# A planned two-layer trunk on one core: latest times, a tie and cold lengths in the plan of the instruction order

## The chip, the cores and the metric

The kernel runs on 1 core of a Trainium2 chip. The metric is the device time of one execution in microseconds (us). Before the change it is 809.21 us, the median of 3 runs (808.96 to 809.29).

## The reference

Two pre-norm residual layers over a sequence of 256 tokens with 1024 channels, all in float32. In each layer one wide projection of the normalised stream feeds three causal token mixers (a Mamba-2 scan, a sliding-window attention with sinks, a forgetting attention). Each mixer's result is projected to 1024 channels, gated and summed. One more projection is added to the residual, and a last RMS norm closes the trunk:

```
for layer in range(DEPTH):                                  # DEPTH = 2
    h = rms_norm(x, norm_w[layer])
    proj = einsum('bsd,de->bse', h, w_in[layer])
    ... split proj: inputs of the three mixers, their gates, the merge gates
    y_a = mamba2_branch(...); y_b = sliding_window_branch(...); y_c = forgetting_attention_branch(...)
    branch = einsum('bsiw,iwd->bsid', stack([y_a, y_b, y_c]), w_proj[layer])
    g = sigmoid(gates + gate_bias[layer])
    x = x + einsum('bsd,de->bse', sum(g * branch), w_out[layer])
return rms_norm(x, final_norm_w)                            # x * rsqrt(mean(x*x) + 1e-6) * w
```

## The kernel before, in words

**Work.** Every large product runs as three fp32r matmuls: each operand is split into a high part (`hi`, a rounding copy on ScalarE) and a remainder (`lo`, a subtraction on VectorE), and high times high, low times high and high times low are summed in PSUM. The 256 tokens are two halves of 128, `t` = 0 and 1. Weights come in parts of 512 KB from HBM on SyncE's queue into `raw`, are split into `hi` and `lo`, and are used once. TensorE's order is the order of the program text and is never changed.

**The plan.** The kernel is not issued as it is written. `Recorder` (line 199) takes down every operation with what it reads and writes, and `Op.cost` (line 159) gives it a length and a lag. `order_of` (line 276) then makes the order of each engine in 7 rounds. A round has two halves. `deadlines` (line 333) goes backwards: every operation gets a latest time `late` and a latest start `due`, from those that need it. A matmul's latest time is its `nominal` time. An operation that nothing on TensorE needs, such as the output's, has its own: `min(op.cap, end + 50.0)` in plan units (meant as us), line 335. `run` (line 351) goes forwards: whenever an engine is free, it takes, of the operations that could begin first, the one with the earliest `due`. `guarded` (line 413) looks whether a more urgent operation becomes ready before the chosen one would be over, and if so the engine takes something short or waits; line 440 uses it only from 16 units on (`OPENING`). The best round by its end is kept, and `emit` (line 498) issues it. So lengths and due times decide only an order; the times on the chip follow from that order and from semaphores.

**Loads are held.** A load without inputs that is not a weight part (line 305) is bound, in the first round, to the matmul that stands `LEAD` = 20 units ahead of its due time, and may not begin earlier in any round.

**The opening.** The program loads `x` half by half, transposes it on TensorE (`turn`, line 1912), and starts the first products. Two groups of transpositions of the identity, 7 (line 1899) and 10 (line 1967), keep TensorE occupied until the data come. In the plan a transposition is 0.109 long. `sum_sq` (line 700) takes the squares from which the first layer's row factor comes; the first projections' evictions are scaled by this factor.

**The end.** In the last layer `u_out2` (line 1653) multiplies the first 256 output columns for both halves, and `u_out` (line 1646) the rest, half by half (512 columns, then 256). `out_end` (line 1670) adds the residual on VectorE, sums the squares, and multiplies the piece by the final norm's weights and -0.5 (line 1687). With the last piece of a half, `row_rsqrt2` (line 711) makes the row factor by a square root on ScalarE, a reciprocal and a refining step on VectorE. Columns 0 to 640 are scaled by it on VectorE and leave on SyncE's queue; the others are scaled on ScalarE and leave on its queue (lines 1694 to 1699). `load_final` (line 1726) loads the weights, broadcast to 128 partitions (512 KB), on ScalarE's queue. The square root needs another activation table than the gates before it. Line 1662 therefore issues a dummy square root into `tab`; `last_of` (line 232) makes it wait for every ScalarE operation recorded before it, loads on ScalarE's queue included. Nothing waits for `tab`.

Of the kernel before, what the change touches and what calls it, by code (L numbers as in the profile page):

```python
# [13 lines left out]
AF = mybir.ActivationFunctionType  # L14
# [36 lines left out]
ENG = mybir.EngineType  # L51
ENGINES = ("tensor", "vector", "scalar", "gpsimd", "sync")
FIRST_WRITES = ("out", "accum_out")
SLIP, OPENING, LEAD = 0.3, 16.0, 20.0


class Buf:
# [79 lines left out]
class Op:  # L137

    def __init__(self, i, engine, name, args, kw):
        self.i, self.engine, self.name, self.args, self.kw = i, engine, name, args, kw  # L140
        self.ins = self
        self.deps, self.behind, self.after, self.bufs = set(), set(), [], []
        views = [("out" if k == 0 else "", a) for k, a in enumerate(args)] + list(kw.items())
        views = [(k, a) for k, a in views if isinstance(a, View)]
        self.writes = [a for k, a in views if k in FIRST_WRITES]
        self.reads = [a for k, a in views if k not in FIRST_WRITES]
        if name == "copy_predicated" or kw.get("accum_op") is not None:
            self.reads += self.writes
        sizes = [a.free_size() for _, a in views] or [1]
        self.cap, self.held = 1e9, False  # L150
        self.dma = name == "dma_start"
        self.n = max(sizes[0:1] if self.dma or engine == "tensor" else sizes)
        if self.dma:
            near = [a for _, a in views if a.buf.on_p][0]
            self.kb = near.shape[0] * near.free_size() / 256
            self.away = 6.0 if engine == "gpsimd" else 5.0
        self.cost()
# [41 lines left out]
class Recorder:  # L199
# [32 lines left out]
    def last_of(self, engine, op):  # L232

        op.deps.update(o.i for o in self.ops if o.engine == engine and o is not op)

    def access(self, op, v, writes):
        b = v.buf
# [38 lines left out]
def order_of(rec, bufs_of, rounds=7, verbose=False):  # L276

    ops = rec.ops
    by_tag = {}
    for b in rec.bufs:  # L280
        by_tag.setdefault(b.tag, []).append(b)
    for op in ops:
        op.behind = [d for d in op.behind - op.deps if ops[d].engine != "tensor" or op.engine != "tensor"]
        op.deps = sorted(op.deps)
        for d in op.deps:
            ops[d].after.append((op, True))
        for d in op.behind:
            ops[d].after.append((op, False))
    before = {}
    for tag, bs in by_tag.items():  # L290
        n = bufs_of[tag]
        for a, b in zip(bs, bs[n:]):
            before[id(b)] = a
    pe = [op for op in ops if op.engine == "tensor"]
    t = 0.0
    for op in pe:
        op.nominal, op.early = t, 0.0
        t += op.busy
    end, best = t, None
    for n in range(rounds):  # L300
        deadlines(ops, before, end)
        if not n:
            at = [op.nominal for op in pe]
            for op in ops:
                if op.dma and not op.deps and op.bufs and op.bufs[0].tag != "raw" and op.due > 10.0:
                    x = pe[bisect.bisect(at, op.due - LEAD) - 1]
                    op.behind.append(x.i)
                    op.held = True
                    x.after.append((op, False))
        end, before = run(ops, by_tag, bufs_of)  # L310
        t = late = last = 0.0
        for op in pe:
            gap, last = op.start - last, op.end
            if op.start > OPENING and gap > 0.03:
                late += gap
                if n > 1:
                    op.early += gap + 0.3
            t = op.start if op.start < OPENING else t
            op.nominal = t
            t += op.busy  # L320
        if best is None or end < best[0]:
            best = (end, [(op.start, op.end) for op in ops], [b.slot for b in rec.bufs])
        if verbose:
            print("round", n, "end", round(end, 2), "late", round(late, 2))
        end = t + 8.0
    for op, (op.start, op.end) in zip(ops, best[1]):
        pass
    for b, b.slot in zip(rec.bufs, best[2]):
        pass
    return sorted(ops, key=lambda op: (op.start, op.i))  # L330


def deadlines(ops, before, end):
    for op in ops:
        op.late = op.nominal + op.busy if op.engine == "tensor" else min(op.cap, end + 50.0)
    for op in reversed(ops):
        op.due = op.late - op.busy
        if op.engine == "tensor":
            op.due = min(op.nominal, op.due) - op.early
        for d in op.deps:  # L340
            o = ops[d]
            o.late = min(o.late, op.due - (o.away if o.dma else o.lag))
        for b in op.bufs:
            a = before.get(id(b))
            if a is not None:
                for o in a.users:
                    if o.i < op.i:
                        o.late = min(o.late, op.due - (o.away if o.dma else o.lag))


def run(ops, by_tag, bufs_of):
# [21 lines left out]
    forced = False  # L373
# [39 lines left out]
    def guarded(e, t0, op):  # L413

        k = 0
        for u in soon[e]:
            if u.due >= min(op.due, t0 + op.busy) or k == 6:
                return None
            if u.start is None and u is not op:
                k += 1  # L420
                r = max(ready_by(u), t0)
                if r < t0 + op.busy and t0 + op.busy > u.due + SLIP:
                    return r
        return None

    while done < len(ops):
        best = None
        for e in ENGINES:
            if e == "tensor":
                if at == len(pe) or pe[at].left:  # L430
                    continue
                c = [(when(pe[at]), pe[at])]
            else:
                c = [(when(op), op) for op in queues[e]]
            c = [(max(r, free[e]), op) for r, op in c if r is not None]
            if not c:
                continue
            t0 = min(r for r, _ in c)
            r, op = min(((r, op) for r, op in c if r <= t0 + 1e-9), key=lambda x: (x[1].due, x[1].i))
            if e != "tensor" and not forced and t0 > OPENING:  # L440
                until = guarded(e, t0, op)
                if until is not None:
                    c = [(r, op) for r, op in c if r + op.busy <= until + 0.02 or op.due < until]
                    if not c:
                        continue
                    t0 = min(r for r, _ in c)
                    r, op = min(((r, op) for r, op in c if r <= t0 + 1e-9), key=lambda x: (x[1].due, x[1].i))
            if best is None or r < best[0]:
                best = (r, e, op)
        if best is None and forced:  # L450
            raise RuntimeError("no operation can begin")
        forced = best is None
        if forced:
            continue
        r, e, op = best
        op.start, op.end = r, r + op.busy
        free[e] = op.end
        if op.dma:
            early = op.start < OPENING
            now, c = op.end + 0.8, op.kb / (330 if early else 300)  # L460
# [55 lines left out]
def hybrid_trunk(  # L516
# [8 lines left out]
    nc = Recorder()  # L525
# [18 lines left out]
    act = nc.scalar.activation  # L544
# [99 lines left out]
    tab = T("tab", [P, 1])  # L644
# [21 lines left out]
    ones = onesr.bitcast(F32)  # L666
# [44 lines left out]
    def row_rsqrt2(v, last):  # L711

        r0 = T("sm", [P, 8])
        if last:
            s = T("sm", [P, 8])
            act(s[:, 0:1], v, AF.Sqrt)
            nc.vector.reciprocal(r0[:, 0:1], s[:, 0:1])
        else:
            nc.gpsimd.tensor_tensor(r0[:, 0:1], v, mhalf[:, 0:1], op=ALU.pow)
        a = T("sm", [P, 8])  # L720
        stt(a[:, 0:1], r0[:, 0:1], v, r0[:, 0:1], op0=ALU.mult, op1=ALU.mult)
        r = T("rs", [P, 8], bufs=4)
        stt(r[:, 0:1], a[:, 0:1], -3.0, r0[:, 0:1], op0=ALU.add, op1=ALU.mult)
        return r
# [21 lines left out]
    def pin(f):  # L746
        return f
# [54 lines left out]
    ops = []  # L802
# [3 lines left out]
    first, late = [], []  # L806
# [846 lines left out]
    def u_out2(y, c):  # L1653

        def f(w):
            def late():
                drain(8)
                limit(None, True)
            drain(7)
            if y.l + 1 == L:  # L1660

                nc.last_of("scalar", pin(act)(tab, ones[:, 0:1], AF.Sqrt))
            xo = [out_start(y, c, t, 0, w.n) for t in range(2)]
            none = lambda: None
            for t, p in enumerate(tok2(y.mh, y.ml, w, (none, late, none, none))):
                out_end(y, c, t, 0, w.n, xo[t], p)
            state["pin"] = False
        return f
# [41 lines left out]
    fin = {}  # L1710
# [181 lines left out]
    if True:  # L1892
# [110 lines left out]
        v = T("sm", [P, 8])  # L2003
# [57 lines left out]
```

## Time and profile before

| what | value |
|---|---|
| median of 3 runs | 809.21 us |
| the profiled execution's own time | 809.29 us |
| its span, first to last instruction | 807.6 us |
| TensorE busy | 795.6 us, 99% |
| VectorE busy | 683.3 us, 85% |
| ScalarE busy | 542.3 us, 67% |
| GpSimd busy | 172.0 us, 21% |
| granted TensorE clock, mean | 0.997 |

How to read the profile's lines: a row of the timeline has the start in us from the span's start, the length in us, the engine, the line of the kernel, the operation, its output and input tiles with their shapes, and how many such instructions stand in a row (x2). In brackets stands how long the engine was idle before it, and what ended that. PE is TensorE's matmul, PEld its weight load, DVE VectorE, ACT ScalarE, POOL GpSimd, SP SyncE; a q behind the name marks the engine's queue, as for the issue of a transfer. All operations carry line 511, the line in `emit` that issues them, so they are told apart by their tiles: `raw`, `hi` and `lo` are weight parts, `mm` and `mx` PSUM banks, `rs` a row factor, `tab` the dummy root's tile, `L` one of the many buffers of common sizes. A row of a group has the count, then the busy time in us and the mean of one in ns.

### The profile page before, as it was taken

To read this page: it belongs to the slowest core of one execution; us is meant where nothing else is said; L and a number is where in the kernel's file an instruction comes from. 1 tells how busy PE (TensorE), PEld (TensorE's weight loads), DVE (VectorE), ACT (ScalarE), POOL (GpSimd) and SP (SyncE) were. 2 spreads that over 40 slices of the span, in tenths; PEclk is the share of its full clock that TensorE was granted. 3 is DMA by queue.
4 is the path that set the end of the run, shared out by engine and by line. 5 is a ranking of instruction groups with operands and counts; after the bars stand their busy time and mean duration, and the time that the engine had idled before them with its cause. 6 is when DMAs were issued, how large, how long until landed. Compare 5 with 4: busy or idle time off the path is not lost.

```text
span 807.6 us, 14854 instructions
## 1 busy us (share of the span) xinstructions
PE 795.6 (99%) x5160; PEld 711.8 (88%) x5160; DVE 683.3 (85%) x1416; ACT 542.3 (67%) x1146; POOL 172.0 (21%) x236
## 2 busy tenths in 40 slices
PE   8999999999999999999999999999999999999995
PEld 8998988888998988888999899888889899888894
DVE  6878999898899996797676889999988999869864
ACT  7876877776766885545466588887666679654442
POOL 2067222130213100031011751212211320002000
PEclk9999999999999999999999999999999999999998
DMA  9899888798944565677688988889886546656622
GB/s 310 270 268 202 252 216 226 204 268 233 251 145 127 183 207 178 191 245 230 200 255 245 259 200 234 200 233 269 237 224 190 182 139 179 211 186 208 224 80 79
DMA packets 138827, 170.43 MB, mean 211 GB/s; under 512 B 9353, under 2 KB 106465, under 8 KB 138753
## 3 DMA queue, kind: packets, MB, share of 16 engines
q1 hardware_dynamic: 114960, 140.53, 56.9%
q0 software_dynamic: 13328, 13.29, 10.0%
q10 hardware_dynamic: 10464, 15.67, 6.5%
q8 instruction: 41, 0.67, 0.3%
q14 instruction: 34, 0.27, 0.1%
HBM read 154.71 MB, written 2.16 MB: 194 GB/s over the span
## 4 chain that ended last, share of the span: by engine, by line
PE 96%; POOL 1%; DVE 1%; issue 1%; DMA 0%; ACT 0%; DVEq 0%; POOLq 0%; ACTq 0%
PE mm L511 83%; PE mx L511 13%; POOL L L511 1%; DVE L L511 1%; DMA L<-in_x_dram 0%; POOL hb L511 0%; POOL qt L511 0%; ACT L L511 0%; DVE pp L511 0%; DVE nm L511 0%; DVE es L511 0%; DVE sm L511 0%; DVEq L2057 0%; POOL nsink L511 0%; ACT sm L511 0%
## 5 line engine op out<-in xcount | busy, mean ns | idle before, releaser
L511 DVE TENSOR_TENSOR lo<-raw,hi 128x1024 fp32r<-128x1024 f32 (+2 forms) x292 | 329.5, 1144 | 47.5 <-ACT hi L511 38.3
L511 PE MATMUL mm<-L,hi 128*128 128x512 f32 x1056 | 354.0, 387 | 0.0
L511 ACT ACTIVATE hi<-raw 128x1024 fp32r<-128x1024 f32 (+2 forms) x292 | 281.2, 977 | 83.3 <-PE mm L511 60.8
L511 PE MATMUL mm<-hi,L 128*128 128x512 f32 (+2 forms) x1168 | 303.3, 349 | 0.1
L511 PE MATMUL mm<-L,lo 128*128 128x256 f32 x1056 | 266.6, 273 | 0.0
L511 PEld LDWEIGHTS mm<-hi,L 128*128 128x128 f32 x1168 | 206.1, 190 | 23.1 <-issue 1.8
L511 PEld LDWEIGHTS mm<-L,hi 128*128 128x128 f32 x1056 | 194.9, 190 | 26.1 <-issue 3.0
L511 PEld LDWEIGHTS mm<-L,lo 128*128 128x128 f32 x1056 | 202.1, 191 | 5.4
L511 PE MATMUL mm<-lo,L 128*128 128x512 f32 (+2 forms) x584 | 201.2, 347 | 0.0
L511 ACT ACTIVATE L<-L 128x256 f32<-128x256 f32 (+2 forms) x184 | 90.0, 504 | 72.7 <-DVE L L511 66.4
L511 PEld LDWEIGHTS mm<-lo,L 128*128 128x128 f32 x584 | 110.2, 190 | 10.7
L511 POOL DMA_DIRECT2D L<-L x80 | 68.0, 900 | 184.2 <-ACT L L511 176.9
L511 ACT ACTIVATE L<-mm 128x256 f32<-128x256 f32 (+2 forms) x202 | 67.4, 373 | 39.0 <-PE mm L511 36.2
L511 DVE TENSOR_TENSOR L<-mm,L 128x256 f32<-128x256 f32 (+1 forms) x70 | 37.2, 535 | 27.0 <-PE mm L511 25.5
L511 POOL TENSOR_SCALAR_AFFINE_SELECT bias<-bias 128x128 f32<-128x128 f32 x64 | 39.0, 707 | 84.3 <-DMA bias<-cumd 84.0
L511 DVE SCALAR_TENSOR_TENSOR L<-L,vec,L 128x254 f32<-128x254 f32 (+3 forms) x112 | 51.9, 478 | 2.2 <-ACT L L511 2.0
L511 ACT ACTIVATE pp<-pp,nm 128x128 f32<-128x128 f32 (+1 forms) x96 | 40.7, 426 | 13.7 <-DVE nm L511 13.5
L511 DVE SCALAR_TENSOR_TENSOR L<-L,L 128x256 f32<-128x256 f32 (+1 forms) x94 | 43.6, 477 | 0.4 <-ACT L L511 0.2
L511 POOL TENSOR_TENSOR sm<-sm,mhalf 128x8 f32<-128x8 f32 (+2 forms) x5 | 7.2, 1435 | 146.4 <-DVE sm L511 146.4
L511 ACT ACTIVATE L<-L,vec 128x256 f32<-128x256 f32 (+1 forms) x48 | 26.8, 566 | 14.2 <-DMA L<-L 14.1
L511 ACT ACTIVATE L<-mx 128x512 f32<-128x512 f32 (+3 forms) x48 | 26.4, 572 | 14.6 <-PE mx L511 14.4
L511 DVE TENSOR_TENSOR L<-L,L 128x512 fp32r<-128x512 f32 (+2 forms) x56 | 33.3, 608 | 0.8 <-ACT L L511 0.2
(139 smaller groups left out, 663.7 us busy)
## 6 DMA issues: line engine op xcount, KB each, us to landing
raw<-in_w_in_dram SPq DMA_DIRECT2D x191, 512.0 KB, 4.9
raw<-in_w_proj_dram SPq DMA_DIRECT2D x48, 512.0 KB, 5.4
L<-L POOLq DMA_DIRECT2D x72, 128.0 KB, 5.3
raw<-in_w_out_dram SPq DMA_DIRECT2D x16, 512.0 KB, 5.3
bias<-cumd ACTq DMA_DIRECT2D x16, 256.0 KB, 4.0
L<-cumd ACTq DMA_DIRECT2D x8, 512.0 KB, 6.3
L<-in_gate_bias_dram ACTq DMA_DIRECT2D x12, 256.0 KB, 4.6
qt<-L POOLq DMA_DIRECT2D x16, 128.0 KB, 5.1
```

Of the source, the lines that this page charges most:

```text
L511: getattr(getattr(nc, op.engine), op.name)(*map(real, op.args), **{k: real(v) for k, v in op.kw.items()})
```

## The change

- The latest time of an operation that nothing on TensorE needs is now `end` instead of `end + 50.0`, and `end` for the next round is TensorE's summed time plus 3.0 instead of 8.0.
- The nominal times of TensorE's operations before 16 units are the bare sum of lengths from 0; from the first operation that starts at 16 or later they go on from that start. Before, each operation of the opening had its own planned start as nominal time.
- `guarded` now acts in the opening too, and hands back the due time of the more urgent operation. What may be taken meanwhile is, besides the short operations, every one that is at least as urgent as that; the older condition (`due` before the time until which is waited) stays only from 16 units on.
- A TensorE operation that starts before 4.9 units (`COLD`) is 1.95 times as long in the plan. Only transpositions stand there.
- The final square root in `row_rsqrt2` depends on the dummy root of line 1662; `last_of` returns the operation for that.
- The landing times of transfers are kept together with the best round's starts.

```diff
-SLIP, OPENING, LEAD = 0.3, 16.0, 20.0
+SLIP, OPENING, LEAD, COLD = 0.3, 16.0, 20.0, 4.9
...
         op.deps.update(o.i for o in self.ops if o.engine == engine and o is not op)
+        return op
...
+        first = True
         for op in pe:
...
-            t = op.start if op.start < OPENING else t
+            if first and op.start >= OPENING:
+                t, first = op.start, False
             op.nominal = t
             t += op.busy
         if best is None or end < best[0]:
-            best = (end, [(op.start, op.end) for op in ops], [b.slot for b in rec.bufs])
+            best = (end, [(op.start, op.end, op.land) for op in ops], [b.slot for b in rec.bufs])
...
-        end = t + 8.0
-    for op, (op.start, op.end) in zip(ops, best[1]):
+        end = t + 3.0
+    for op, (op.start, op.end, op.land) in zip(ops, best[1]):
...
-        op.late = op.nominal + op.busy if op.engine == "tensor" else min(op.cap, end + 50.0)
+        op.late = op.nominal + op.busy if op.engine == "tensor" else min(op.cap, end)
...
                 if r < t0 + op.busy and t0 + op.busy > u.due + SLIP:
-                    return r
+                    return r, u.due
...
-            if e != "tensor" and not forced and t0 > OPENING:
+            if e != "tensor" and not forced:
                 until = guarded(e, t0, op)
                 if until is not None:
-                    c = [(r, op) for r, op in c if r + op.busy <= until + 0.02 or op.due < until]
+                    until, due = until
+                    c = [(r, op) for r, op in c if r + op.busy <= until + 0.02 or op.due <= due
+                         or t0 > OPENING and op.due < until]
...
-        op.start, op.end = r, r + op.busy
+        op.start, op.end = r, r + op.busy * (1.95 if e == "tensor" and r < COLD else 1.0)
...
-            act(s[:, 0:1], v, AF.Sqrt)
+            act(s[:, 0:1], v, AF.Sqrt).deps.add(fin["root"].i)
...
-                nc.last_of("scalar", pin(act)(tab, ones[:, 0:1], AF.Sqrt))
+                fin["root"] = nc.last_of("scalar", pin(act)(tab, ones[:, 0:1], AF.Sqrt))
```

More of the change, by code (lines that the diff above doesn't have):

```diff
@@ L149, in __init__ @@
         sizes = [a.free_size() for _, a in views] or [1]
-        self.cap, self.held = 1e9, False
+        self.cap, self.held, self.land = 1e9, False, None
         self.dma = name == "dma_start"
```

## The prediction

> **What bounds the kernel now.** I read the page first, then the chain of waits, then the timeline engine by engine at both ends of the span, and last the answers for the two transfers that concern the end. The chain of waits by line:
>
> ```profile
> core 0 of [0], span 807.6 us
> by line: PE mm L511 82.7%; PE mx L511 12.9%; issue 0.8%; POOL L L511 0.6%; DVE L L511 0.6%; DMA L<-in_x_dram 0.4%; POOL hb L511 0.4%; POOL qt L511 0.3%; ACT L L511 0.2%; DVE pp L511 0.2%; DVE nm L511 0.1%; DVE es L511 0.1%; DVE sm L511 0.1%
> ```
>
> The chain that ends last is TensorE for 95.6% (82.7 and 12.9) of 807.6 us. The diff takes no matmul away and changes no matmul's place in TensorE's order, so only what lies before TensorE's first work, behind its last, and in its waits can move. The end is where most of that is. VectorE's part of it, from the timeline of that engine:
>
> ```profile
> 792.28 0.16 DVE L511 SCALAR_TENSOR_TENSOR rs<-sm,sm 128x1 f32<-128x1 f32 x1
> ...
> 797.33 0.15 DVE L511 TENSOR_SCALAR sm<-sm 128x1 f32<-128x1 f32 x1
> 798.33 0.42 DVE L511 TENSOR_TENSOR L<-mm,L 128x256 f32<-128x256 f32 x1 [0.85 <-PE mm L511]
> ...
> 800.14 0.16 DVE L511 SCALAR_TENSOR_TENSOR rs<-sm,sm 128x1 f32<-128x1 f32 x1
> 800.22 2.63 DVE L511 SCALAR_TENSOR_TENSOR L<-L,L 128x512 f32<-128x512 f32 x6
> 802.76 1.01 DVE L511 TENSOR_SCALAR L<-L,rs 128x640 f32<-128x640 f32 x2
> ```
>
> The add at 798.33 waited for TensorE, so TensorE's last matmul is over at about 798.3 and 9.3 us of the span lie behind it. Of those, 2.0 us go to the last row factor `rs` (798.33 to 800.30): add, sum of squares, square root, reciprocal, two small steps. Each needs the one before. Then come six multiplications by the final norm's weights and two by the row factors. Six of those are two token halves times three column pieces, and five of the six have had their input for a long time. Why they wait is in the answer for the weights' load:
>
> ```profile
> L511 ACTq DMA_DIRECT2D L<-in_final_norm_w_dram x1: 339/339/339, 796.4 to 796.4; - x1
> ...
> DMA to landing us min/median/max: 3.7/3.7/3.7
> ```
>
> It is issued at 796.4 and lands near 800.1. The code says why it is so late: its only users are the output's operations, these have `end + 50` as their latest time, and a load without inputs is held, in the first round, behind the matmul that stands 20 plan units ahead of its due time. With 50 added, that is the last matmul of all. ScalarE and the output's transfers:
>
> ```profile
> 799.56 0.19 ACT L511 ACTIVATE tab<-ones 128x1 f32<-128x1 f32 x1
> 801.88 1.12 ACT L511 ACTIVATE L<-L,rs 128x384 f32<-128x384 f32 x2 [2.13 <-DVE L L511]
> 802.52 0.85 ACTq L511 DMA_DIRECT2D out_dram<-L  x2
> ```
>
> Both token halves leave together at the very end, although half 0 had its row factor at 792.44, long before TensorE was done with half 1.
>
> **The change part by part.**
>
> *Latest time of the output's operations.* In the first round the load's due time becomes TensorE's end less what follows it (a multiplication, a scaling, an output issue, 5.0 for the load itself): about 7.4 before the end. It is held behind the matmul 20 ahead of that, some 27 us before TensorE's end, near 771. It costs ScalarE's queue 0.34 us there, and 3.7 us of landing are hidden by more than 20. The multiplications become ready piece by piece. The five early ones then run in VectorE's waits, the latest of them, half 1's 512 columns, behind 797.33 + 0.15 = 797.48 and before the add at 798.33. That leaves 0.85 us for it. The forms of the tail, grouped:
>
> ```profile
> L511 DVE SCALAR_TENSOR_TENSOR L<-L,L 128x256 f32<-128x256 f32 x4 | 1.4, 420 | 0.0
> L511 DVE SCALAR_TENSOR_TENSOR L<-L,L 128x512 f32<-128x512 f32 x2 | 1.3, 686 | 0.0
> ...
> L511 DVE TENSOR_SCALAR L<-L,rs 128x640 f32<-128x640 f32 x2 | 1.0, 548 | 0.0
> ```
>
> Neighbours overlap, so I price by starts. The six start between 800.22 and 802.76, that is 2.54 us for four short and two long ones, and a long one costs 0.27 more (686 less 420). So 6a + 0.53 = 2.54: a short one 0.335, a long one 0.60. The long one fits in 0.85 us. One short one stays behind the last add. So 2.54 - 0.335 = 2.205 us leave the end. Of the two scalings one, half 0's, leaves too: 1.01 - 0.55 = 0.46 us. VectorE's last result comes at 803.77 - 2.205 - 0.46 = 801.10, which is 2.67 us earlier.
>
> The writes behind it. Traffic over 798 to 808, forty slices of 0.25 us:
>
> ```profile
> DMA  9997120000000000000004999999999950000000
> GB/s 377 360 279 115 66 98 16 0 0 0 0 0 0 0 0 0 0 0 0 0 0 154 362 387 375 381 365 430 389 400 369 399 185 0 0 0 0 0 0 0
> ```
>
> (The first six slices hold the end of the weights' load.) The output's 1024 KB flow without a pause from 803.25 to 806.2, at some 385 GB/s, starting 0.7 us behind the first issue at 802.52. With half 0 gone 512 KB are left, some 1.35 us. From the new last scaling: 801.10 + 0.7 + 1.35 = 803.15, against 806.2: 3.05 us earlier. If instead each transfer took as long as now, it would be the 2.67. I take 2.9, nearer the sum by bytes, because the row shows the engines at 9 of 10 for the whole stretch. The answer for the output gives the landing of the four:
>
> ```profile
> DMA to landing us min/median/max: 1.9/2.2/2.8
> ```
>
> The Trainium skill ("DMA: Bandwidth & Descriptors", the latency of one DMA) has a fixed 2.0 us beside bytes over 436 GB/s. By it a 320 KB write takes an estimated 2.75 us however few are beside it, and the gain would be the 2.67. The row's 2.8 for the slowest and 1.9 for the quickest do not decide between the two.
>
> *The table's tie.* The dummy square root `tab` now has a user, so it gets a due time. It waits for every earlier operation recorded on ScalarE, and that includes the weights' load; this is why it came at 799.56, behind the real square roots that it should prepare. With the load early it becomes ready when half 0's last transposed split is done. ScalarE there:
>
> ```profile
> 779.36 1.08 ACT L511 ACTIVATE hi<-raw 128x1024 fp32r<-128x1024 f32 x1 [1.78 <-issue]
> 780.32 0.60 ACT L511 ACTIVATE L<-mx 128x512 fp32r<-128x512 f32 x1
> ...
> 789.26 1.28 ACT L511 ACT_TABLE_LOAD   x1
> ```
>
> The table load of 1.28 us moves from 789.26, where ScalarE has nothing to do, into the gap of 1.78 us before 779.36. Hidden before, hidden after: 0, and its cover is a gap only 0.5 us longer than it is. If the tie put it behind 779.36 instead, the split at 780.32 would move by 1.28 and TensorE, whose next matmuls take this split, with it. Bounds 0 to +1.28; I take 0.
>
> The opening's load of the other table, on the same engine:
>
> ```profile
> 1.43 1.28 ACT L511 ACT_TABLE_LOAD   x1 [1.43 <-PEq L2050]
> 2.73 0.20 ACT L511 ACTIVATE tab<-tab 128x1 f32<-128x1 f32 x1
> ```
>
> The next activation starts 1.30 us after the load starts, so nothing more than the 1.28 is paid. The Trainium skill ("ScalarE: Activation LUTs", What ACT_TABLE_LOAD costs) speaks against the tie: it adds a drain of 1.38 us to each switch, 2.66 in all. By that figure an estimated 0.9 us of it would stick out of the gap of 1.78. No drain shows in this row.
>
> *The opening: the guard, the compact nominal times, the cold transpositions.* Before 16 plan units an idle engine may now wait for a more urgent operation, due times there follow TensorE's bare order, and transpositions before 4.9 count double. TensorE's weight loads show where it waits once real work runs:
>
> ```profile
> 12.25 0.52 PEld L511 LDWEIGHTS mm<-hi,L 128*128 128x128 f32 x4 [0.30 <-ACT L L511]
> 12.98 0.52 PEld L511 LDWEIGHTS mm<-hi,L 128*128 128x128 f32 x4 [0.21 <-DVE L L511]
> ```
>
> There is 0.5 us to win at most, and both waits are latencies of a chain (transposition, multiply, copy, subtract) whose engines start each step at once. The reorder that I see is the rope table's load going behind the third weight part, because its cap of 8 is no longer the most urgent due time. Nobody waits for either. I take 0, bounds -0.5 to the +1.5 of the second rival.
>
> Sum: 807.6 - 2.9 = 804.7 of span. The profiled run takes 809.29, 1.69 more than its span, so 806.4. The median of the three runs is 0.08 below that run: 806.3.
>
> **The rivals.**
>
> *First: the output stays late.* If the load were still held to the end, or its buffer came free late, nothing would move: 809.2. For it speaks that only the first round places the hold. Against it, that round's `end` is the sum of TensorE's lengths, and nothing is added to it now. A lesser form: half 1's long multiplication misses its 0.85 us, and 0.6 of the 2.9 stays: 806.9; this lies within the forecast's range.
>
> *Second: the guard pushes the squares of token half 1 behind the weight splits of the opening.* The row factor of the first layer hangs on them.
>
> ```profile
> 10.66 0.61 ACT L511 ACTIVATE L<-L 128x512 f32<-128x512 f32 x1
> ...
> 13.66 2.34 ACT L511 ACTIVATE hi<-raw 128x512 fp32r<-128x512 f32 x3
> ...
> 19.75 0.47 ACT L511 ACTIVATE L<-mm,rs 128x256 f32<-128x256 f32 x1 [0.81 <-DVE rs L511]
> ```
>
> ```profile
> 20.56 0.30 PEld L511 LDWEIGHTS mm<-hi,L 128*128 128x128 f32 x2
> ```
>
> The eviction at 19.75 waits for `rs` and ends at 20.22; the third projection starts at 20.56 in the bank that it frees, so the slack is 0.34. With both squares behind the splits, which end at 16.0, they would end at 16.0 + 2 x 0.61 = 17.2 instead of 11.3. The factor's next steps do not follow the squares at once today: they wait for VectorE's own splits until shortly before 16. So the factor would come by my estimate 1.8 us late, and TensorE 1.8 - 0.34 = 1.5 late: 807.8. For it: the second square sits right in front of the copy of half 1 that TensorE waits for at 12.25, so a small error of the plan makes a collision. Against it: in the trace it ends before that copy's input is there, and the guard acts only on a collision.
>
> *Third: the table load lands in front of the split at 780.32.* Then TensorE loses the load's length, 1.28 us, and 807.6 comes out. For it: the plan counts the dummy root as a short operation, not as 1.28 us, so nothing keeps it away from a spot without cover. Against it: it has the least urgent due time on ScalarE, and the first idle spot behind its inputs is the long gap. By the drain that the Trainium skill states (the page named above) the same split would be late by the estimated 0.9 us even from the gap, an estimated 807.2.
>
> *Fourth, on the other side: GpSimd's queue ahead of the first attention.*
>
> ```profile
> 74.86 0.35 DVE L511 CUSTOM_DVE_ANT_0 pp<-mx,wmask,nsink 128x128 f32<-128x128 f32 x1 [1.04 <-POOL nsink L511]
> ```
>
> ```profile
> 77.84 0.87 POOL L511 DMA_DIRECT2D L<-L  x1
> ```
>
> ```profile
> 78.48 0.63 PE L511 MATMUL mx<-ident,pp 128*128 128x128 f32 x4 [0.32 <-DVE es L511]
> ```
>
> VectorE waits 1.04 us for the negated sinks, which stand in GpSimd's queue among accumulating transfers, and TensorE waits 0.32 us for what follows. There is no slack. If the plan, re-decided after a changed opening, puts such transfers ahead of the sinks, each costs TensorE its 0.87 us. Four eat the gain (3.5 against 2.9) and give 809.8; six give 811.5. For it: the queue is in order and the chain has no cover. Against it: due times there come from TensorE's order, which stays.
>
> **How the numbers follow.** About 0.2%, or 1.6 us, is what a measurement of this kernel can tell from no change. Forecast 0.80: the tail shrinks by 2.3 to 3.4 (3.05, and another 0.335 if the short multiplication finds room in the square root's wait), the opening gives 0 to -0.5: 805.3 to 806.9. First rival 0.04, second 0.07, third 0.05, fourth 0.04. The first (809.2), the second (807.8) and the third (807.6) lie no more than 1.6 us below 809.2: 0.16 for the same. Slower 0.04, faster the forecast's 0.80. The range takes in the third, since the forecast alone just holds 8 in 10 and its edges are bounds and not measurements: 805.3 to 807.6, with 0.15 outside.
>
> **What would show it.** In the changed profile the weights' load is issued near 771, five multiplications by it stand before TensorE's end and one behind, half 0's two output transfers are issued before TensorE's end, the output's traffic at the end lasts about 1.4 us instead of 3, and 6.4 us lie behind TensorE's last matmul instead of 9.3. The table load stands in the gap before 779.36. TensorE's last matmul still ends near 798.3; if that moved by over 0.7 us either way, the opening or the order in the middle did it, and my zero there is wrong. If the load still stands behind the last matmul, the first step is wrong.

## The result, and the profile after

The changed kernel takes 806.11 us, the median of 6 runs (805.52 to 806.63). The kernel before, run beside it, takes 808.93 us (6 runs, 808.72 to 809.29). The ratio is 0.9964, 95% interval 0.9952 to 0.9975: faster by 2.8 us. The profiled execution takes 805.79 us with a span of 804.1; what lies around the span is 1.69 us as before. All operations now carry line 516.

The end of the chain of waits of the changed kernel (start in us, length in us, what):

```profile
775.63 0.44 PE mx L516 x4
...
778.75 0.44 PE mx L516 x4
779.19 18.61 PE mm L516 x120
```

TensorE's last matmul is over at 779.19 + 18.61 = 797.80, 0.50 earlier than before, and 804.1 - 797.8 = 6.3 us lie behind it, where 9.3 lay. So 3.0 of the span's 3.5 come from the tail and 0.5 from TensorE's own way there. (The medians show 2.8 and not 3.5: the profiled execution of the kernel before is the slowest of its six, that of the changed kernel the second fastest.) The tail, on VectorE's timeline:

```profile
784.33 0.75 DVE L516 SCALAR_TENSOR_TENSOR L<-L,L 128x256 f32<-128x256 f32 x2
...
788.83 0.68 DVE L516 SCALAR_TENSOR_TENSOR L<-L,L 128x512 f32<-128x512 f32 x1
...
790.96 0.42 DVE L516 SCALAR_TENSOR_TENSOR L<-L,L 128x256 f32<-128x256 f32 x1
...
791.96 0.55 DVE L516 TENSOR_SCALAR L<-L,rs 128x640 f32<-128x640 f32 x1
...
796.69 0.68 DVE L516 SCALAR_TENSOR_TENSOR L<-L,L 128x512 f32<-128x512 f32 x1
...
797.82 0.42 DVE L516 TENSOR_TENSOR L<-mm,L 128x256 f32<-128x256 f32 x1 [0.38 <-PE mm L516]
...
798.82 0.42 DVE L516 SCALAR_TENSOR_TENSOR L<-L,L 128x256 f32<-128x256 f32 x1
799.17 0.16 DVE L516 RECIPROCAL sm<-sm 128x1 f32<-128x1 f32 x1
...
799.62 0.16 DVE L516 SCALAR_TENSOR_TENSOR rs<-sm,sm 128x1 f32<-128x1 f32 x1
799.82 0.55 DVE L516 TENSOR_SCALAR L<-L,rs 128x640 f32<-128x640 f32 x1
```

Five multiplications by the final weights stand ahead of the add at 797.82, and the sixth, at 798.82, stands in the wait for the square root: the reciprocal behind it starts when the root is there. The last result comes at 799.82 + 0.55 = 800.37, that is 2.57 behind TensorE's end, where it was 803.77 - 798.30 = 5.47. The answer for the weights' load (its issue, then issue to landing):

```profile
L516 ACTq DMA_DIRECT2D L<-in_final_norm_w_dram x1: 339/339/339, 766.8 to 766.8; - x1
...
DMA to landing us min/median/max: 6.4/6.4/6.4
```

Issued at 766.8, landed near 773.2, first used at 784.33. ScalarE's timeline shows where the table load went, and that half 0's output leaves at 792.6:

```profile
777.08 1.28 ACT L516 ACT_TABLE_LOAD   x1
778.37 0.20 ACT L516 ACTIVATE tab<-ones 128x1 f32<-128x1 f32 x1
778.84 1.08 ACT L516 ACTIVATE hi<-raw 128x1024 fp32r<-128x1024 f32 x1 [0.26 <-ACT tab L516]
...
792.60 0.35 ACTq L516 DMA_DIRECT2D out_dram<-L  x1
```

The split at 778.84 starts 0.35 us ahead of the last 120 matmuls (779.19); before it was 779.36 against 779.71, the same 0.35. Nothing was pushed. The output's traffic over 794 to 805, in GB/s for forty slices of 0.275 us:

```profile
GB/s 371 350 298 30 30 20 17 0 0 0 0 0 0 0 0 0 0 0 0 0 0 0 0 0 0 0 242 410 361 385 352 157 0 0 0 0 0 0 0 0
```

Half 0's traffic is over before TensorE's end (the first columns), and half 1's is a block of its own. Summed and divided by the mean rate of its full slices (377), it lasts 1907 x 0.275 / 377 = 1.39 us. With the part-filled first and last slices counted by their share it runs from 801.25 to 802.64.

### The profile page after: what moved, and what is told of

Same layout as the page of the kernel before. It is cut to its first block, busy times and chain, and to the rows that moved or that the text cites. A ratio compares the mean times of both kernels' runs of the same rounds, so it can differ in the third digit from the quotient of the medians.

```text
span 804.1 us, 14862 instructions
## 1 busy us (share of the span) xinstructions
PE 795.5 (99%) x5160; PEld 711.3 (88%) x5160; DVE 682.9 (85%) x1416; ACT 540.9 (67%) x1146; POOL 171.7 (21%) x236
## 4 chain that ended last, share of the span: by engine, by line
PE 97%; DVE 1%; DMA 1%; ACT 0%; POOL 0%; issue 0%; SPq 0%; ACTq 0%
PE mm L516 84%; PE mx L516 13%; DMA raw<-in_w_in_dram 1%; DVE L L516 0%; DVE pp L516 0%; ACT L L516 0%; DVE es L516 0%; SPq L516 0%; DVE nm L516 0%; POOL L L516 0%; ACT hi L516 0%; POOL hb L516 0%; POOL nsink L516 0%; DVE sm L516 0%; DVE rs L516 0%
## 5 line engine op out<-in xcount | busy, mean ns | idle before, releaser
L516 POOL TENSOR_SCALAR_AFFINE_SELECT bias<-bias 128x128 f32<-128x128 f32 x64 | 36.5, 627 | 87.7 <-DMA bias<-cumd 82.7
L516 DVE SCALAR_TENSOR_TENSOR L<-L,vec,L 128x255 f32<-128x255 f32 (+3 forms) x112 | 51.4, 476 | 2.5 <-ACT L L516 2.2
```

What stands on the lines that cost most here:

```text
L516: getattr(getattr(nc, op.engine), op.name)(*map(real, op.args), **{k: real(v) for k, v in op.kw.items()})
```

## The experiments

Eight kernels were run, the first four beside the kernel before at 809.19 us (21 runs), the others beside it at 809.27 us (21 runs). The changed kernel's 806.11 is from the session of the result, where the kernel before took 808.93. The theory was the prediction's: all of the gain comes from the final weights' load being held less, which frees VectorE's multiplications and half 0's output from the tail. The main rival was that the opening's part (guard, compact nominal times, cold lengths) or the tie has a share.

**early_load.** The kernel before, where only this one load is held 50 units further ahead. Nothing else of the change is in it.

```diff
+fin_buf = [None]
...
-                    x = pe[bisect.bisect(at, op.due - LEAD) - 1]
+                    x = pe[bisect.bisect(at, op.due - LEAD - (50.0 if op.bufs[0] is fin_buf[0] else 0.0)) - 1]
...
         fin["w"] = T("L4", [P, D])
+        fin_buf[0] = fin["w"].buf
```

> The kernel before with one edit: the final norm's weights are held behind the matmul 70 plan units ahead of their due time instead of 20, which puts them where the change puts them. All latest times stay at end + 50. Theory (the held load is the whole of the tail): 2.7 to 3.1 us less than before, TensorE's last matmul ends at the same 798.3, 6.3 us lie behind it. Rival (the due times do it, or the opening does): less than 1.5 us, with multiplications left behind the last matmul or the gain missing.

It takes 806.21 us, ratio 0.9962 (0.995 to 0.9975). The changed kernel's whole gain is there. On its chain of waits, TensorE's last piece, and on ScalarE's timeline the table load:

```profile
779.90 18.60 PE mm L512 x120
```

```profile
777.78 1.28 ACT L512 ACT_TABLE_LOAD   x1
```

TensorE ends at 798.50, and with a span of 804.8 there are 6.3 us behind it, as in the changed kernel. The table load falls into the same gap without any tie: the dummy root had only been waiting for the weights' load. So the gain is the hold of one load, and the other parts of the diff are not needed for it.

**opening_only.** The change without its late part: `end + 50.0` and `t + 8.0` are back, and there is no tie.

```diff
-        end = t + 3.0
+        end = t + 8.0
...
-        op.late = op.nominal + op.busy if op.engine == "tensor" else min(op.cap, end)
+        op.late = op.nominal + op.busy if op.engine == "tensor" else min(op.cap, end + 50.0)
...
-            act(s[:, 0:1], v, AF.Sqrt).deps.add(fin["root"].i)
+            act(s[:, 0:1], v, AF.Sqrt)
```

> The changed kernel with the latest time back at end + 50, the next round's end at 8.0 and without the tie: the guard, the compact nominal times and the cold lengths alone. Theory (they are worth nothing): within 0.3 us of before. Rival (the 0.5 us by which TensorE ends earlier in the changed profile come from them): 0.4 to 0.8 us less than before, TensorE's last matmul ends at 797.5 to 797.9.

It takes 809.13 us, ratio 0.9997 (0.9988 to 1.0006): nothing that can be measured, though the interval leaves room for 1.0 us less and 0.5 more. In its profile TensorE ends at 797.67, 0.6 earlier than before, with a span of 806.9 and 9.2 us behind TensorE's end. The tail is the old one. What its earlier TensorE end is worth is taken up below.

**tie_only.** The kernel before with the tie alone.

```diff
+        return op
...
-            act(s[:, 0:1], v, AF.Sqrt)
+            act(s[:, 0:1], v, AF.Sqrt).deps.add(fin["root"].i)
...
-                nc.last_of("scalar", pin(act)(tab, ones[:, 0:1], AF.Sqrt))
+                fin["root"] = nc.last_of("scalar", pin(act)(tab, ones[:, 0:1], AF.Sqrt))
```

> The kernel before with the tie alone: the final square roots depend on the dummy root. Theory (the table load had cover before): no gain, 0 to 0.8 us more than before, since the dummy root still waits for the held load and now drags the table load and half 0's row factor behind the last 512 columns' square. Rival (the table load was part of the end): 1.0 to 1.3 us less.

It takes 810.58 us, ratio 1.0016 (1.0008 to 1.0025): slower by 1.4 us, more than was expected. ScalarE's and VectorE's timelines show how:

```profile
796.09 0.34 ACTq L512 DMA_DIRECT2D L<-in_final_norm_w_dram  x1
...
796.82 1.28 ACT L512 ACT_TABLE_LOAD   x1
...
803.49 0.86 ACTq L512 DMA_DIRECT2D out_dram<-L  x2
```

```profile
799.72 0.69 DVE L512 SCALAR_TENSOR_TENSOR L<-L,L 128x512 f32<-128x512 f32 x1 [0.60 <-DMA L<-in_final_norm_w_dram]
800.33 0.15 DVE L512 RECIPROCAL sm<-sm 128x1 f32<-128x1 f32 x1
...
802.65 0.23 DVE L512 SCALAR_TENSOR_TENSOR rs<-sm,sm 128x1 f32<-128x1 f32 x2
```

The tie makes the real square roots wait for the dummy, and the dummy for ScalarE's operations before it, the load's issue at 796.09 among them. So half 0's root, too, is taken only behind the table load. Its reciprocal then stands on VectorE behind a multiplication that waits for the landing, and the row factors are ready at 802.88 instead of 800.30. ScalarE's outputs are issued at 803.49, where it was 802.52. The tie is harmless only once the load is early.

**old_filter.** The change, but in the main part an engine that waits may take only what the older condition allowed.

```diff
-                    c = [(r, op) for r, op in c if r + op.busy <= until + 0.02 or op.due <= due
+                    c = [(r, op) for r, op in c if r + op.busy <= until + 0.02 or t0 <= OPENING and op.due <= due
```

> The changed kernel, but from 16 plan units on the guard's choice is the old one (a more urgent operation that comes later is not let through). Theory (the order in the middle moves TensorE by some tenths either way): 805.6 to 806.8, with the wait near 78 or near 472 there or gone. Rival (the wider choice itself is worth something): 0.5 to 1 us more than the changed kernel's 806.1.

It takes 806.35 us, ratio 0.996 (0.9947 to 0.9972), the same as the change. The order in the middle differs nevertheless: a wait of TensorE in layer 1 (472.28 in the change, shown below) isn't there, and another one is, ahead of the last group of transpositions. TensorE's weight loads:

```profile
779.16 0.42 PEld L516 LDWEIGHTS mx<-ident,L 128*128 128x128 f32 x4 [0.36 <-DVE L L516]
```

The condition only moves waits of a few tenths about.

**out_together.** The change, but half 0's two output transfers are issued behind half 1's. All of VectorE's and ScalarE's work stays where the change has it, so this measures the bytes alone.

```diff
-                    ts(y.xn[:, t, 0:m], y.xn[:, t, 0:m], r[:, 0:1], None, op0=ALU.mult)
-                    nc.sync.dma_start(out2[t * P:(t + 1) * P, 0:m], y.xn[:, t, 0:m])
-                    act(y.xn[:, t, m:D], y.xn[:, t, m:D], AF.Copy, scale=r[:, 0:1])
-                    nc.scalar.dma_start(out2[t * P:(t + 1) * P, m:D], y.xn[:, t, m:D])
+                    a = ts(y.xn[:, t, 0:m], y.xn[:, t, 0:m], r[:, 0:1], None, op0=ALU.mult)
+                    b = act(y.xn[:, t, m:D], y.xn[:, t, m:D], AF.Copy, scale=r[:, 0:1])
+                    if t == 1:
+                        for u in (1, 0):
+                            nc.sync.dma_start(out2[u * P:(u + 1) * P, 0:m], y.xn[:, u, 0:m]).deps.add(a.i)
+                            nc.scalar.dma_start(out2[u * P:(u + 1) * P, m:D], y.xn[:, u, m:D]).deps.add(b.i)
```

> The changed kernel, but half 0's two output transfers are issued behind half 1's, at the very end; everything else in its order is the changed kernel's. It prices the writes. Theory (the end is bound by bytes, about 385 GB/s): the 512 KB more add 1.1 to 1.4 us to the changed kernel's 806.1, so 807.2 to 807.6, and the traffic at the end lasts about 3 us. Rival (a fixed time per transfer, however many there are): only the second issue's 0.36 us, 806.5.

It takes 807.46 us, ratio 0.9979 (0.9971 to 0.9988), 1.35 more than the changed kernel's median. Measured against the kernel before of its own session it gains 1.81 instead of 2.82, which makes the difference 1.0. TensorE ends at 798.01, so 805.8 - 798.0 = 7.8 us lie behind it instead of 6.3. The traffic over 794 to 806, slices of 0.3 us:

```profile
GB/s 0 0 0 0 0 0 0 0 0 0 0 0 0 0 0 0 0 0 0 0 0 0 0 0 60 375 365 358 379 406 381 389 364 357 62 0 0 0 0 0
```

By the same reckoning it flows for 2.80 us against 1.39: the second 512 KB cost 1.41 us of traffic. This decides between the prediction's two readings of the writes. The Trainium skill's fixed 2.0 us and bytes over 436 GB/s ("DMA: Bandwidth & Descriptors", Anatomy of one DMA — SWDGE (gpsimd) path) is a fit for one transfer that GpSimd issues, and these are issued by SyncE and ScalarE. Taken for each transfer by itself, as the prediction took it, the two later ones would add only their issue, an estimated 0.5 us (0.84 for two on a queue against 0.36 for one). The row decides for the bytes: the four transfers that are out together move some 375 GB/s in all.

**table_between.** The change, with the dummy root forced between a split of weights and the copy of the transposed half that TensorE waits for next: the third rival's place.

```diff
+            fin["turned", c, t] = nc.ops[-2]
...
+    parts_hi = [o for o in nc.ops if o.engine == "scalar" and o.writes and o.writes[0].buf.tag == "hi"]
+    fin["root"].deps.add(parts_hi[-2].i)
+    fin["turned", 512, 1].deps.add(fin["root"].i)
```

> The changed kernel with the dummy root forced behind the weight split of 779.36 and in front of the transposed split that TensorE waits for (positions of the profile before). It prices the third rival. Theory (a table load costs its 1.28 us and nothing more, and there is no cover here): 1.1 to 1.5 us more than the changed kernel, TensorE's last matmul later by as much. Rival (a drain of 1.38 us beside it): 2.5 to 2.8 us more. Rival (cover somewhere): 0.

It takes 807.95 us, ratio 0.9982 (0.9973 to 0.9991): 1.84 more than the changed kernel's median, or 1.5 when each is measured against the kernel before of its own session. ScalarE's timeline, and TensorE's weight load that waits for the copy:

```profile
779.40 1.08 ACT L516 ACTIVATE hi<-raw 128x1024 fp32r<-128x1024 f32 x1 [1.78 <-issue]
780.49 1.28 ACT L516 ACT_TABLE_LOAD   x1
781.78 0.20 ACT L516 ACTIVATE tab<-ones 128x1 f32<-128x1 f32 x1
781.89 0.58 ACT L516 ACTIVATE L<-mx 128x512 fp32r<-128x512 f32 x1
```

```profile
782.52 0.19 PEld L516 LDWEIGHTS mm<-hi,L 128*128 128x128 f32 x1 [1.62 <-ACT L L516]
```

The copy starts 2.49 behind the split (781.89 against 779.40), where in the change it is 0.98 (779.82 against 778.84): 1.51 more. TensorE's load waits 1.62 us, and TensorE ends at 799.86. The span is 2.1 longer than the change's, of which 0.56 was there already before this place (the four transpositions that start at 775.63 in the change start at 776.19); 1.5 is the price of the place. The load takes 1.29 us from its start to the next activation, and it starts 0.01 behind the split's end: the drain of 1.38 us that the Trainium skill puts on every switch ("ScalarE: Activation LUTs", What ACT_TABLE_LOAD costs) shows on neither side of it.

**sinks_early.** The change, with the five small loads of the head constants (`hb`) held 35 instead of 20 units ahead. They stand in GpSimd's queue ahead of the negated sinks, the fourth rival's place.

```diff
-                    x = pe[bisect.bisect(at, op.due - LEAD) - 1]
+                    x = pe[bisect.bisect(at, op.due - LEAD - getattr(op, "sooner", 0.0)) - 1]
...
-            pdma(y.hb[:, 16 * i:16 * i + 16], v[l:l + 1, :].to_broadcast([P, 16]))
+            o = pdma(y.hb[:, 16 * i:16 * i + 16], v[l:l + 1, :].to_broadcast([P, 16]))
+            o.cap = 1e9
+            o.sooner = 15.0
```

(The line with `cap` sets the value that these loads have anyway.)

> The changed kernel with the five small loads of each layer's head constants, the sinks among them, held 35 instead of 20 plan units ahead. Theory (the wait of about 0.3 us for the negated sinks, in layer 0 before and in layer 1 after, is GpSimd's queue): the wait for what follows the sinks is gone in both layers, 0.2 to 0.4 us less than the changed kernel, which the timing may just not show. Rival (the wait has another end behind it): no change within 0.3 us.

It takes 805.59 us (805.49 to 805.79), ratio 0.9955 (0.9942 to 0.9967): the lowest median of all kernels here, though its interval overlaps the change's. The wait in layer 1, on TensorE's timeline of the change and then of this kernel:

```profile
471.76 0.38 PE L516 MATMUL mm<-L,hi 128*128 128x512 f32 x1
472.28 0.63 PE L516 MATMUL mx<-ident,pp 128*128 128x128 f32 x4
```

```profile
471.81 0.38 PE L516 MATMUL mm<-L,hi 128*128 128x512 f32 x1
472.03 0.60 PE L516 MATMUL mx<-ident,pp 128*128 128x128 f32 x4
```

Starts in a row stand 0.22 apart here and 0.52 there. From the 268 matmuls of layer 1 to the last 120, this kernel takes 778.90 - 411.50 = 367.40 us, the change 779.19 - 411.44 = 367.75.

The wait is gone, but in layer 1 it was not a wait for the sinks. VectorE waits 0.15 us for them in the change, and also 0.15 in old_filter, where TensorE has no wait here. What differs is a small operation on the chain behind them, `es`, and what GpSimd does beside it. VectorE's and GpSimd's timelines of the change, then VectorE's of old_filter:

```profile
468.66 1.68 DVE L516 TENSOR_TENSOR es<-nm,nsink 128x4 f32<-128x4 f32 x1
```

```profile
468.56 1.75 POOL L516 TENSOR_TENSOR qt<-L,L 128x256 f32<-128x256 f32 x2
```

```profile
468.87 0.16 DVE L516 TENSOR_TENSOR es<-nm,nsink 128x4 f32<-128x4 f32 x1
```

In the change `es` starts 0.10 behind the start of GpSimd's pair and ends 0.03 behind its end. In old_filter no such pair runs beside it. The kernels part cleanly: in the five that have TensorE's wait in layer 1 (the change, opening_only, out_together, table_between, out_split) this `es` takes 1.66 to 1.72 beside the pair, and in the other five at most 0.16. So this kernel's order of GpSimd's work took the pair away from `es` (0.16 at 468.16, the pair at 469.41). That VectorE is held up by the pair is read from these rows; no run moved the pair alone.

**out_split.** The change, with each half's output in four pieces instead of two, so that the first traffic starts sooner.

```diff
-                    ts(y.xn[:, t, 0:m], y.xn[:, t, 0:m], r[:, 0:1], None, op0=ALU.mult)
-                    nc.sync.dma_start(out2[t * P:(t + 1) * P, 0:m], y.xn[:, t, 0:m])
-                    act(y.xn[:, t, m:D], y.xn[:, t, m:D], AF.Copy, scale=r[:, 0:1])
-                    nc.scalar.dma_start(out2[t * P:(t + 1) * P, m:D], y.xn[:, t, m:D])
+                    for a, b in ((0, 320), (320, m)):
+                        ts(y.xn[:, t, a:b], y.xn[:, t, a:b], r[:, 0:1], None, op0=ALU.mult)
+                        nc.sync.dma_start(out2[t * P:(t + 1) * P, a:b], y.xn[:, t, a:b])
+                    for a, b in ((m, 832), (832, D)):
+                        act(y.xn[:, t, a:b], y.xn[:, t, a:b], AF.Copy, scale=r[:, 0:1])
+                        nc.scalar.dma_start(out2[t * P:(t + 1) * P, a:b], y.xn[:, t, a:b])
```

> The changed kernel with each half's output scaled and sent in four pieces instead of two. Theory (the writes' bytes bound the end, and they can start when the first piece is scaled): traffic starts about 0.25 us earlier, 0.2 to 0.4 us less than the changed kernel. Rival (a fixed time per transfer and the issues bound it): 0 to 0.4 us more.

It takes 806.28 us, ratio 0.9963 (0.995 to 0.9977): no gain. The traffic over 794 to 806, slices of 0.3 us:

```profile
GB/s 139 9 17 172 358 321 44 0 0 0 0 0 0 0 0 0 0 0 0 0 0 0 0 30 333 332 346 347 314 46 0 0 0 0 0 0 0 0 0 0
```

It starts at 801.17, 3.27 behind TensorE's end (797.90) where the change has 3.45, and its full slices hold 314 to 347 GB/s instead of 352 to 410. It ends 4.84 behind TensorE's end, as in the change. The lower rate takes back what the earlier start brings. Whether the shorter rows (1280 and 768 bytes instead of 2560 and 1536) or the greater number of transfers lower it was not separated.

## Why the prediction was right, point by point

806.3 was forecast and 806.11 measured, a gain of 2.9 against 2.8 between the medians. The mechanism is shown: one load's hold, by early_load; the sizes are compared step by step.

**The load.** Foreseen near 771, issued at 766.8, and landed in 6.4 us instead of 3.7 beside weight parts. Neither mattered: 11 us were left until its first use at 784.33.

**The multiplications and the scaling: the mis-sized term.** The prediction had 2.205 + 0.46 = 2.67 and left one short multiplication (0.335) behind the last add. That one found room in the wait for the square root (798.82, shown above); the edge of the forecast, 3.4, had allowed for it. Add to row factor is as long as before: 797.82 to 799.78, 1.96, against 798.33 to 800.30, 1.97. So by the prediction's prices 3.00 should have gone. 2.90 went: before, the first multiplication overlapped the row factor by 0.08, and the scaling that follows it now starts 0.04 behind the factor's end.

**The writes.** By bytes the prediction expected VectorE's gain and another 0.38. Bytes do set the price, as out_together shows with 1.41. Yet the span's part behind VectorE's last result shrank only from 3.83 to 3.73. The prediction read edges of slices as the traffic's ends. Counted by share, the traffic before ran from 803.40 to 806.12, and it starts 0.88 behind the first issue (802.52), in the change 0.85 (800.40). The working had 0.7 for this. Seen from VectorE's last result, 1.33 us of traffic went (2.72 less 1.39) and 1.25 came back: in the kernel before ScalarE's pieces were issued 1.25 us ahead of that result (802.52 against 803.77), so the 0.88 and the first 0.37 of the traffic lay beside VectorE's work, and now both queues start at the very end. Against the full sum by bytes, 3.05, the two errors (0.23 too little on VectorE, 0.28 too much on the writes) nearly cancel, which is luck: 2.90 and 0.10 make the 3.0 measured. The 2.9 that the prediction took lay between its two readings.

**The table and its tie.** The load stands in the gap, and costs nothing, as foreseen. But the step gave the credit to the wrong edit. early_load has the same place without the tie, and its time agrees with the change's within 0.1 us. The change without the tie was not run.

**The opening.** Zero was taken, and opening_only shows nothing measurable. In the profiles TensorE's end moved by -0.50, inside the 0.7 that was allowed, as a sum of three. The start of the 72 matmuls of the opening went from 23.76 to 23.48, but kernels with the old opening's order have 23.61 to 24.10 and those with the new one 23.38 to 24.03, so this part is scatter. The chains of waits hold the rest, of the kernel before and then of the changed one:

```profile
23.76 13.04 PE mm L511 x72
...
78.48 0.63 PE mx L511 x4
79.11 5.40 PE mm L511 x40
...
412.23 45.83 PE mm L511 x268
```

```profile
23.48 13.04 PE mm L516 x72
...
77.87 0.44 PE mx L516 x4
78.31 5.40 PE mm L516 x40
...
411.44 45.76 PE mm L516 x268
```

From the 72 matmuls to the 40 it was 79.11 - 23.76 = 55.35 and is 78.31 - 23.48 = 54.83: the wait of 0.32 at 78.48 is gone, and the four transpositions take 0.44 instead of 0.63. That recurs in every kernel with the new opening. In layer 1 the same place (472.28, shown with sinks_early) went the other way, beside the long `es`, and from the 268 matmuls to the last 120 it was 779.71 - 412.23 = 367.48 and is 367.75. Whether the -0.52 and +0.27 are worth anything in the time is open: the medians of opening_only and before differ by 0.06.

**The rivals.** The first fell: the load moved. The second did not occur, as the 72 matmuls start no later. The third's place was not taken; forced there it costs 1.5, and it had been priced at 1.28. It left out the dummy root itself and the handing over. The fourth was right that GpSimd's order is where the plan moves TensorE, and in layer 0 VectorE's wait for the sinks did shrink, from 1.04 us to 0.15. Its price was wrong: 0.5 us in layer 0 one way and 0.3 in layer 1 the other, not 0.87 for each of several transfers. In layer 1 its mechanism was wrong too: the time goes where `es` runs beside GpSimd's pair, not in a transfer ahead of the sinks.

## What to carry to other kernels

When many operations at a kernel's end look like a bound of their engine, look for one late input that holds them all: here the plan kept a 512 KB load to the last matmul, and its hold alone was worth 3 us. Price the tail by what remains exposed and not by what leaves: what the early issue of a transfer had hidden comes back when that transfer goes, and a wait on the chain itself (a square root on another engine) can take a short operation for free. An edit that is harmless in a set, like the tie, can cost 1.4 us alone, because it hangs on the condition that another edit removes.

## What the runs showed of the hardware beside this

The first transpositions of the opening take almost twice as long as eight of the same form 6 us later, at the same granted clock. TensorE's timeline of the changed kernel, and the row of the first stretch with the granted clock in the column before the last two:

```profile
3.59 1.97 PE L516 MATMUL mx<-ident,L 128*128 128x128 f32 x8 [0.20 <-DMA L<-in_x_dram]
5.36 1.77 PE L516 MATMUL mx<-ident 128*128 128x128 f32 x10
...
9.92 1.04 PE L516 MATMUL mx<-ident,L 128*128 128x128 f32 x8
```

```profile
1.00:5.00 4.00, 3.36 (x15) 2.89 (x16) 0.42 (x2) 2.87 (x6) 1.91 (x11) 1.00 0.69 218
```

Eight take 1.97 us at 3.59 and 1.04 at 9.92, a factor of 1.9, near the plan's 1.95. The ten in between take 1.77, a pace between the two. The column shows 1.00 all the while, also from 9.90 to 10.80. What slows the first ones isn't seen in the clock's column, and no run here was made for it.
